# Three unread fp32 matmuls behind the modulation sums of the first two rows

## The chip, the cores and the metric

The kernel runs on one core of one Trainium2 chip. The time is device time in microseconds (us) of one launch. Of the kernel before there are three timed runs, and one more execution that was profiled; the rows below come from that one.

## The reference

One decoder layer over 512 positions of width 1024, in fp32. Its head, where the change sits, is this:

```python
mod = c @ w_ada[l] + b_ada[l]
sh1, sc1, gt1, sh2, sc2, gt2 = jnp.split(mod, 6, axis=-1)
h = rms_norm(x, g_pre_mix[l]) * (1.0 + sc1[:, None]) + sh1[:, None]
proj = h @ w_in[l]
```

Behind it come two groups of attention heads (one with compressed, selected and sliding-window branches, one with a top-k choice of keys), one output projection, a gated residual, a second modulated norm, and a squared-ReLU feed-forward of width 4096. Every value of the output depends on `proj`.

## The kernel before

The 1024 model columns are eight rows of 128, `k` = 0 to 7. For each row the head does the same things. The modulation weights of the row (`wm`, 1 MB) are loaded; PE multiplies them by the vector `c` (`mod_sums`, L286) into one PSUM bank, tile `mp`; ACT copies the partial sums to `macc` (L292); PE adds them up with two matmuls of one column each (`mod_mm`, L297), which write columns 256 and 257 of the same bank. DVE adds the bias (L301) and applies the norm's gain (L302): these are the row's scale and shift. With them ACT writes the high half of the modulated row, `hh` (L305); DVE computes the same row in full (L307) and subtracts `hh` from it, which gives the low half, `hl` (L308). The projection is done in three passes over high and low halves (`proj_pass`, L324): weights high (`uh`) with `hh`, weights low (`ul`) with `hh`, weights high with `hl`. The weights are halved by `split` (ACT at L123, DVE at L124). Two chunks of `w_in` columns run this way, A (452 columns, accumulators `pA`, four of them) and B (512 columns, `pB`, three of them, one row later). The first row's transposed input is `xT_0`; the others are made by PE transposes (`xTp`, L269) and copied by ACT or DVE (L270). Four of the transposes use the banks that `pA` takes over later.

The order on each engine is set by a scheduler that simulates the program with its own durations while the kernel is built. `tc.issue_after` holds an instruction behind another on its engine. Waits between engines are derived from the tiles; in the built program a reader of a PSUM bank waits for every matmul that the code writes into that bank ahead of it. The scheduler's order covers the whole program, so a change in the head can also move rows much later: the attention stage (about 100 to 390 us) mixes score matmuls (L886, L887), their row minima on DVE (L889, which free the four score banks), softmax scalings (L907), and the top-k search on DVE (MAX8 at L576, MATCH_REPLACE8 at L579, in rounds).

Of the kernel before, what the change touches and what calls it, by code (L numbers as in the profile page):

```python
# [69 lines left out]
def layer_kernel(  # L70
# [7 lines left out]
    V, A, G, PE, SY = nc.vector, nc.scalar, nc.gpsimd, nc.tensor, nc.sync  # L78
# [23 lines left out]
    def p2(name, dt=F32):  # L102
        return big.tile([P, 512], dt, tag="p2", name=name, bufs=N_P)
# [77 lines left out]
    ident = identr.bitcast(F32)  # L181
# [82 lines left out]
    xT = [p2(f"xT_{k}") for k in range(KT)]  # L264
# [29 lines left out]
    def mod_mm(k):  # L294
        ps, acc = macc[k]
        for v in range(2):
            mm = PE.matmul(ps[:, 256 + v:257 + v], acc[:, v, :], ones32, start=True, stop=True)  # L297
        return ps[:, 256:258], mm

    def mod_h(k, ps):  # L300
# [20 lines left out]
    def proj_pass(ps, t, k, w, n, i):  # L321
        hi, lo = w[k // 2]
        l, r = ((hh, hi), (hh, lo), (hl, hi))[i]
        return PE.matmul(ps[:, :n], l[:, t, k, :], r[:, k % 2, :n],  # L324
                         start=(k == 0 and i == 0), stop=(k == KT - 1 and i == 2))
# [8 lines left out]
    def behind(done, f, *args):  # L334

        with ExitStack() as es:
            for ins in done:
                es.enter_context(tc.issue_after(ins.ins))
            return f(*args)

    first = mod_sums(0)
    first_T = x_transpose(0, "S")
    mp, _ = mod_mm(0)
    behind((first, first_T), split_a, 0)
    rt_ops = rope_tables()
    psB = []
    for k in range(KT):
# [18 lines left out]
        for ps in (0, 1, 2):  # L366
            for t in range(NT):
                mm = proj_pass(psA[t], t, k, wA, 452, ps)
# [13 lines left out]
        if k + 1 < KT:  # L382
            mp, mm = behind((mm,), mod_mm, k + 1)
# [940 lines left out]
```

## Time and profile before

| what | value |
|---|---|
| median of three runs | 724.51 us (720.13 to 725.61) |
| profiled execution, its own time | 724.97 us |
| its span, first to last instruction | 723.2 us |
| mean granted TensorE clock | 0.967 |
| PE busy | 674.7 us (93%) |
| DVE busy | 510.3 us (71%) |
| ACT busy | 373.9 us (52%) |
| POOL busy | 191.9 us (27%) |

The span is 1.8 us shorter than the execution's own time, which also holds what lies around the first and last instruction. The granted clock is a share of full speed: 1.00 is 2.4 GHz and 0.50 is 1.2 GHz.

### The profile page before, as it was taken

To read this page: it belongs to the slowest core of one execution; us is meant where nothing else is said; L and a number is where in the kernel's file an instruction comes from. 1 tells how busy PE (TensorE), PEld (TensorE's weight loads), DVE (VectorE), ACT (ScalarE), POOL (GpSimd) and SP (SyncE) were. 2 spreads that over 40 slices of the span, in tenths; PEclk is the share of its full clock that TensorE was granted. 3 is DMA by queue.
4 is the path that set the end of the run, shared out by engine and by line. 5 is a ranking of instruction groups with operands and counts; after the bars stand their busy time and mean duration, and the time that the engine had idled before them with its cause. 6 is when DMAs were issued, how large, how long until landed. Compare 5 with 4: busy or idle time off the path is not lost.

```text
span 723.2 us, 10022 instructions
## 1 busy us (share of the span) xinstructions
PE 674.7 (93%) x3529; PEld 523.1 (72%) x3529; DVE 510.3 (71%) x1020; ACT 373.9 (52%) x755; POOL 191.9 (27%) x228
## 2 busy tenths in 40 slices
PE   3999989899998999799978999999999999999994
PEld 2678968777565676365668878888888888888883
DVE  5555458988997989775686539677597459695445
ACT  5343785435795669544464555433554355454221
POOL 3000285734523134222020022201140032231023
PEclk9899989999997999999999999999999999999998
DMA  9976630530316471462295212452144312322103
GB/s 293 311 232 188 199 88 1 117 116 30 118 30 191 133 171 30 117 233 87 65 339 156 90 54 85 145 178 57 29 146 146 116 30 58 88 88 93 53 1 116
DMA packets 91611, 87.15 MB, mean 121 GB/s; under 512 B 3909, under 2 KB 71593, under 8 KB 91562
## 3 DMA queue, kind: packets, MB, share of 16 engines
q1 hardware_dynamic: 91170, 86.46, 39.7%
q8 instruction: 28, 0.46, 0.3%
q14 instruction: 21, 0.17, 0.1%
q10 hardware_dynamic: 392, 0.06, 0.0%
HBM read 84.40 MB, written 2.10 MB: 120 GB/s over the span
## 4 chain that ended last, share of the span: by engine, by line
PE 74%; DVE 14%; DMA 4%; ACT 3%; POOL 2%; issue 2%; POOLq 0%; DVEq 0%; ACTq 0%; SPq 0%
PE up L1126 23%; PE dn L1254 15%; PE dn L1187 5%; PE op L1019 5%; PE pA L324 3%; PE O L918 3%; PE pB L324 2%; PE pj_E L324 2%; DVE wk L579 1%; PE pj_D L324 1%; DVE m L576 1%; DMA rwo_b<-in_w_out_dram 1%; DMA wg_g<-in_w_ada_dram 1%; PE tp_d L912 1%; PE pj_C L324 1%
## 5 line engine op out<-in xcount | busy, mean ns | idle before, releaser
L1126 PE MATMUL up<-hh,uh_U 128*128 128x512 f32 (+1 forms) x288 | 105.9, 369 | 3.2 <-ACT hh L123 2.7
L1126 PE MATMUL up<-hl,uh_U 128*128 128x512 f32 (+1 forms) x288 | 104.8, 369 | 1.0 <-DVE hl L124 1.0
L1126 PE MATMUL up<-hh,ul_U 128*128 128x512 f32 (+1 forms) x288 | 105.5, 368 | 0.0
L1216 POOL TENSOR_TENSOR r<-r,r 128x512 f32<-128x512 f32 x18 | 36.8, 2055 | 184.6 <-ACT r L1131 114.0
L123 ACT CAST th<-rd 128x1024 fp32r<-128x1024 f32 x42 | 44.2, 1053 | 75.1 <-PE dn L1254 40.6
L124 DVE TENSOR_TENSOR tl<-rd,th 128x1024 fp32r<-128x1024 f32 x42 | 53.9, 1288 | 39.4 <-ACT th L123 39.4
L124 DVE TENSOR_TENSOR ul_U<-rw_U,uh_U 128x1024 fp32r<-128x1024 f32 x32 | 43.1, 1346 | 32.8 <-ACT uh_U L123 32.6
L1126 PEld LDWEIGHTS up<-hh,uh_U 128*128 128x128 f32 x288 | 54.9, 191 | 12.7 <-ACT hh L123 3.2
L1126 PEld LDWEIGHTS up<-hl,uh_U 128*128 128x128 f32 x288 | 54.5, 191 | 10.0 <-DVE hl L124 1.2
L1126 PEld LDWEIGHTS up<-hh,ul_U 128*128 128x128 f32 x288 | 54.9, 191 | 8.7
L123 ACT CAST uh_U<-rw_U 128x1024 fp32r<-128x1024 f32 x32 | 33.6, 1049 | 50.9 <-PE up L1126 32.3
L1254 PE MATMUL dn<-th,sl 128*128 128x512 f32 x168 | 52.1, 391 | 0.3
L1254 PE MATMUL dn<-th,sh 128*128 128x512 f32 x168 | 51.9, 393 | 0.0
L1254 PE MATMUL dn<-tl,sh 128*128 128x512 f32 x168 | 51.7, 389 | 0.0
L1254 PEld LDWEIGHTS dn<-th,sh 128*128 128x128 f32 x168 | 31.5, 188 | 7.5 <-DVE usum L1241 0.6
L1254 PEld LDWEIGHTS dn<-th,sl 128*128 128x128 f32 x168 | 31.3, 188 | 7.6 <-DVE sl L124 1.2
L1254 PEld LDWEIGHTS dn<-tl,sh 128*128 128x128 f32 x168 | 31.5, 188 | 6.6
L1216 DVE TENSOR_TENSOR rd<-rd,rd 128x1024 f32<-128x1024 f32 x24 | 31.5, 1324 | 0.3
L123 ACT CAST sh<-r 128x512 fp32r<-128x512 f32 x42 | 25.2, 619 | 9.0 <-POOL r L1216 8.6
L124 DVE TENSOR_TENSOR sl<-r,sh 128x512 fp32r<-128x512 f32 x42 | 27.9, 710 | 0.0
L1241 DVE TENSOR_TENSOR y<-y,dn 128x512 f32<-128x512 f32 x40 | 25.5, 680 | 2.2 <-PE dn L1254 2.2
L576 DVE MAX8 m<-wk 128x8 f32<-128x256 f32 (+2 forms) x48 | 26.5, 552 | 0.7 <-POOL wk L571 0.4
(426 smaller groups left out, 1685.2 us busy)
## 6 DMA issues: line engine op xcount, KB each, us to landing
rw_U<-in_w_up_dram SPq DMA_DIRECT2D x32, 512.0 KB, 4.1
rd<-in_w_down_dram SPq DMA_DIRECT2D x24, 512.0 KB, 4.7
wm<-in_w_ada_dram SPq DMA_DIRECT2D x32, 256.0 KB, 6.1
x<-in_x_dram SPq DMA_DIRECT2D x8, 512.0 KB, 6.5
wv_g<-in_w_ada_dram SPq DMA_DIRECT2D x8, 512.0 KB, 6.9
rwo_a<-in_w_out_dram SPq DMA_DIRECT2D x16, 256.0 KB, 4.5
wv_a<-in_w_ada_dram SPq DMA_DIRECT2D x8, 512.0 KB, 4.0
rwo_b<-in_w_out_dram SPq DMA_DIRECT2D x16, 256.0 KB, 4.7
```

Source lines behind the costliest of these rows:

```text
L123: A.copy(hi, src)
L124: eng.tensor_tensor(lo, src, hi.bitcast(F32), op=OP.subtract)
L324: return PE.matmul(ps[:, :n], l[:, t, k, :], r[:, k % 2, :n], start=(k == 0 and i == 0), stop=(k == KT - 1 and i == 2))
L576: mx = V.max(m8, work[t])
L579: V.match_replace(work[t], m8, work[t], MARK)
L918: mm = [PE.matmul(O[j][g * 64:(g + 1) * 64, :], vn[kb][:, self.vsl[g]:self.vsl[g] + 64], pts[kb, g][0], start=(first and kb == 0), stop=(l ...
L1019: PE.matmul(stt["ps"], l[:, kk, :], r[:, kk % 2, :], start=(kk == 0 and i == 0), stop=(kk == 7 and i == 2))
L1126: PE.matmul(pv[:, t0:t1, :], l[:, k, :], r[:, t0:t1, k, :], start=(n == 0), stop=(n == 23))
L1187: PE.matmul(ps, l[:, t * P:(t + 1) * P], r[:, f % 2, :], start=(n == 0), stop=(n == 11))
L1216: eng.tensor_tensor(dst, x, y, op=op)
L1241: V.tensor_tensor(ya, ya, ps, op=op)
L1254: PE.matmul(ps[t], l[:, f, t * P:(t + 1) * P], r[:, f, :], start=(n == 0), stop=(n == 11))
```

## The change

After the two sums of rows 0 and 1, PE multiplies 252 columns of `xT_0` by the identity three times, in fp32, into columns 258 to 509 of the same bank. Nothing reads the result. `mod_mm` now returns the last of the three as its instruction, so what was issued behind the sum is issued behind that.

```diff
@@ -295,6 +295,10 @@
         ps, acc = macc[k]
         for v in range(2):
             mm = PE.matmul(ps[:, 256 + v:257 + v], acc[:, v, :], ones32, start=True, stop=True)
+        if k < 2:
+            with tc.issue_after(mm.ins):
+                for _ in range(3):
+                    mm = PE.matmul(ps[:, 258:510], ident, xT[0][:, 0:252], start=True, stop=True)
         return ps[:, 256:258], mm
```

From here on lines have numbers that are 4 higher in the changed kernel (L301 becomes L305).

The engines' orders move with it. First place: DVE in the head, from the first row's scale and shift to the second row's. Before:

```order
L301 TENSOR_TENSOR as_174<-mp_187,colb 128x2
L302 TENSOR_TENSOR as_174<-as_174,colT 128x1
L307 TENSOR_SCALAR h_0_213<-xT_164,as_174 128x512
L124 TENSOR_TENSOR ulA_207<-rwA_92,uhA_206 128x2x452
L308 TENSOR_TENSOR hl_173<-h_0_213,hh_172 128x4x128
L270 COPY xT_165<-xTp_217 128x512
L270 COPY xT_167<-xTp_229 128x512
L270 COPY xT_169<-xTp_280 128x512
L301 TENSOR_TENSOR as_174<-mp_255,colb 128x2
L302 TENSOR_TENSOR as_174<-as_174,colT 128x1
L124 TENSOR_TENSOR ulB_271<-rwB_175,uhB_270 128x1024
L307 TENSOR_SCALAR h_1_296<-xT_165,as_174 128x512
```

The same stretch of DVE after the change:

```order
L124 TENSOR_TENSOR ulA_210<-rwA_92,uhA_209 128x2x452
L305 TENSOR_TENSOR as_174<-mp_187,colb 128x2
L306 TENSOR_TENSOR as_174<-as_174,colT 128x1
L311 TENSOR_SCALAR h_0_216<-xT_164,as_174 128x512
L312 TENSOR_TENSOR hl_173<-h_0_216,hh_172 128x4x128
L270 COPY xT_165<-xTp_220 128x512
L270 COPY xT_167<-xTp_232 128x512
L270 COPY xT_169<-xTp_283 128x512
L124 TENSOR_TENSOR ulB_274<-rwB_175,uhB_273 128x1024
L305 TENSOR_TENSOR as_174<-mp_258,colb 128x2
L306 TENSOR_TENSOR as_174<-as_174,colT 128x1
L311 TENSOR_SCALAR h_1_302<-xT_165,as_174 128x512
```

In both rows the weights' low half (`ulA`, then `ulB`) now stands ahead of the add that makes the scale and shift; before it stood behind.

Second place: PE around the first row's sums. Before:

```order
L297 MATMUL mp_187<-ones_109,macc_196 128x1 x2
L324 MATMUL pA_235<-uhA_206,hh_172 128x452
L324 MATMUL pA_236<-uhA_206,hh_172 128x452
L324 MATMUL pA_235<-ulA_207,hh_172 128x452
L324 MATMUL pA_236<-ulA_207,hh_172 128x452
L324 MATMUL pA_235<-uhA_206,hl_173 128x452
```

PE there after the change:

```order
L297 MATMUL mp_187<-ones_109,macc_196 128x1 x2
L301 MATMUL mp_187<-xT_164,identr 128x252 x3
L328 MATMUL pA_238<-uhA_209,hh_172 128x452
L328 MATMUL pA_238<-ulA_210,hh_172 128x452
L328 MATMUL pA_239<-uhA_209,hh_172 128x452
L328 MATMUL pA_239<-ulA_210,hh_172 128x452
L328 MATMUL pA_238<-uhA_209,hl_173 128x452
```

The three unread matmuls stand between the sums and the first projection matmul, and two of the projection's matmuls change places; the second row gets the same three, with no other move on PE.

Third place: DVE at the start of the top-k search of the second query block (`wk` is the score table that is searched, `sk_kw` a split of window keys, `peT` a table that PE transposes for the compression). Before:

```order
L576 MAX m_1_1422<-wk_687 128x8
L579 MATCH_REPLACE wk_687<-m_1_1422,wk_687 128x256
L613 COPY peT<-pep_k 128x16
L576 MAX m_1_1449<-wk_687 128x8
L579 MATCH_REPLACE wk_687<-m_1_1449,wk_687 128x256
L576 MAX m_1_1476<-wk_687 128x8
L579 MATCH_REPLACE wk_687<-m_1_1476,wk_687 128x256
```

After:

```order
L580 MAX m_1_1428<-wk_693 128x8
L583 MATCH_REPLACE wk_693<-m_1_1428,wk_693 128x256
L580 MAX m_1_1455<-wk_693 128x8
L583 MATCH_REPLACE wk_693<-m_1_1455,wk_693 128x256
L580 MAX m_1_1482<-wk_693 128x8
L583 MATCH_REPLACE wk_693<-m_1_1482,wk_693 128x256
L617 COPY peT<-pep_k 128x16
```

Two rounds of the search have moved ahead of the copy of `peT`. Beyond these places the same instructions stand on every engine, with some dozens of rows in other places between about 100 and 390 us.

## Rows read from the trace of the kernel before

**Rows 1.** The page's part on the chain that ended last, by engine.

```profile
PE 74%; DVE 14%; DMA 4%; ACT 3%; POOL 2%; issue 2%; POOLq 0%; DVEq 0%; ACTq 0%; SPq 0%
```

**Rows 2.** The chain in the head: start us, us, what.

```profile
17.04 0.82 ACT hh L305
...
17.91 4.20 PE pA L324 x11
22.10 1.54 PE mp L286 x16
...
24.04 0.94 ACT uhB L123
...
26.24 3.19 PE pA L324 x8
...
30.67 0.59 PE xTp L269 x4
...
32.41 2.17 PE pB L324 x9
34.58 1.00 PE mp L286 x16
35.58 2.67 PE pA L324 x12
38.25 0.34 PE mp L297 x4
```

**Rows 3.** PE in order of time, head: start, us; idle before and its releaser.

```profile
17.91 0.94 PE L324 MATMUL pA<-uhA,hh 128*128 128x452 f32 x2 [2.22 <-ACT hh L305]
...
26.24 1.68 PE L324 MATMUL pA<-uhA,hh 128*128 128x452 f32 x4 [1.46 <-ACT hh L305]
```

**Rows 4.** Stretches of the head; the third column from the right is the granted clock.

```profile
19.60:19.70 0.10, 0.10 (x2) 0.00 (x0) 0.10 (x1) 0.00 (x0) 0.00 (x0) 0.82 1.09 277
23.00:23.10 0.10, 0.10 (x8) 0.08 (x4) 0.00 (x0) 0.00 (x0) 0.00 (x0) 0.61 1.17 349
26.40:26.50 0.10, 0.10 (x1) 0.10 (x2) 0.10 (x1) 0.00 (x0) 0.00 (x0) 0.95 1.11 348
29.80:30.00 0.20, 0.20 (x8) 0.17 (x4) 0.00 (x0) 0.00 (x0) 0.00 (x0) 0.74 1.15 289
```

**Rows 5.** DVE in order of time, head.

```profile
16.45 0.23 DVE L243 TENSOR_SCALAR rtab<-rtab 128x128 f32<-128x128 f32 x1
...
17.50 1.09 DVE L124 TENSOR_TENSOR ulA<-rwA,uhA 128x904 fp32r<-128x904 f32 x1
18.51 0.69 DVE L308 TENSOR_TENSOR hl<-h,hh 128x512 fp32r<-128x512 f32 x1
19.11 1.88 DVE L270 COPY xT<-xTp 128x512 f32<-128x512 f32 x3
...
25.16 1.23 DVE L124 TENSOR_TENSOR ulB<-rwB,uhB 128x1024 fp32r<-128x1024 f32 x1
```

**Rows 6.** PE at 179 us: two records of one full-width fp32 matmul.

```profile
179.49 1.02 PE L758 MATMUL gv_g<-bb,ones 128*128 128x512 f32 x2
```

**Rows 7.** A stretch with idle PE; columns as in rows 4, PE's busy time first.

```profile
369.90:385.00 15.10, 10.17 (x77) 9.04 (x76) 14.73 (x28) 7.68 (x18) 3.26 (x4) 1.00 0.81 255
```

**Rows 8.** DVE in the top-k search, in order of time.

```profile
107.76 0.43 DVE L576 MAX8 m<-wk 128x8 f32<-128x256 f32 x1 [0.40 <-POOL wk L571]
...
108.30 0.41 DVE L579 MATCH_REPLACE8 wk<-m,wk 128x256 f32<-128x256 f32 x1
...
111.75 0.17 DVE L613 COPY peT<-pep_k 128x16 f32<-128x16 f32 x1 [2.06 <-PE pep_k L611]
```

**Rows 9.** PE in the attention stage, behind two of its longer stalls.

```profile
144.58 0.50 PE L324 MATMUL pj_E<-uh_E,hh 128*128 128x512 f32 x1 [3.09 <-DVE mx L889]
...
221.36 0.44 PE L886 MATMUL s_s<-k1s,qC 128*128 128x384 f32 x1 [2.06 <-DVE mx L889]
```

**Rows 10.** Two stretches behind those stalls; columns as in rows 4.

```profile
146.00:149.30 3.30, 3.30 (x9) 2.52 (x9) 3.30 (x12) 0.86 (x4) 1.75 (x3) 0.50 0.01 2
...
224.50:234.70 10.20, 10.20 (x43) 6.20 (x40) 6.40 (x19) 4.22 (x10) 3.29 (x2) 0.50 0.70 228
```

## Prediction

> **What bounds the kernel.** I read the page's chain first: 74% of the span is PE [rows 1], so a shift of PE's work in the head goes on to the end unless a later stall swallows it. Then I followed the chain through the head. It runs PE, then the modulation chain, then PE, twice: hh of row 0 on ACT at 17.04, eleven projection matmuls from 17.91, the sums of row 1 from 22.10 to 23.64, the weights' cast on ACT to 24.98, and PE again at 26.24. From there it stays on PE [rows 2]. So there are just two gaps, of 2.22 and 1.46 us, and both end with hh [rows 3]. Last I looked at the granted clock: it falls from 1.00 to 0.50 (2.4 to 1.2 GHz) near 19.67, comes back near 23.06, falls again at 26.49 and is back by 29.9 [rows 4]. Each fall comes after one of the gaps, when PE is already at work again. The reader should see the price of the low clock: eight projection matmuls take 3.19 from 26.24, 0.40 each, twelve take 2.67 from 35.58, 0.22 each; the sums take 1.54 at 22.10 and 1.00 at 34.58 [rows 2].
>
> **The change, part by part.**
>
> *The unread matmuls themselves.* The nearest row is a full-width fp32 matmul of 512 columns: two records in 1.02, the second starting about 0.43 after the first, so 0.86 a matmul [rows 6]. 252 columns are 0.42, three are 1.27. The bounds are half of that, if the weights' second half cost nothing, and 2.5 at the low clock. I take 1.27, since the clock stands at 1.00 when both gaps begin. Row 0's three then run from about 15.6 to 16.9 and row 1's from 24.7 to 26.0, within PE's idle time [rows 3]. xT_0 is copied before the sums need their operand, so they add no new wait of PE's own, and no DMA moves in the head.
>
> *What they keep waiting.* They write the bank that DVE's add (L301) reads. In the built program the counter of PE that the add waits for is stepped by the third of them; before, the second sum stepped it. So the scale and shift of the row come behind all three. The Trainium skill has the rule behind this, in "PSUM — Partial Sum Buffer", section "PSUM bank collisions raise a hardware error": "Semaphore-guard PSUM by bank × quadrant (by bank is the simple version), not by address." By address the add would wait for the sums alone and the gaps would stay as they are; by the rule they grow. No run here shows the two side by side.
>
> *The first gap, +0.3.* The scheduler has put ulA ahead of the add (first place in the orders). DVE is busy with the angle tables until 16.68, and ulA takes 1.09 [rows 5]; it ends near 17.7, after the unread matmuls, and hides them. The add, hh and PE all come 1.09 later: hh at 18.13, PE at 19.0 in place of 17.91. If the unread matmuls ran at the low clock they would end near 18.2 and cost another 0.5. ulA no longer stands between hh and hl, so hl ends at 19.7 in place of 19.20 and the three xT copies, whose banks the third and fourth accumulators take, come 0.5 later, not 1.09 [rows 5]. What matters is that PE is idle from about 16.95 to 19.0: 2.05 us in place of 2.22. The idle time is moved, not removed. I therefore take the same fall of the clock at 19.67. Of the eleven matmuls three run before it, eight take 0.40 each, to 22.9; the sums begin at the low clock and end, with the clock back near 23.06, at 23.95. Before they ended at 23.64 [rows 2]. That is +0.3.
>
> *The second gap, +1.25.* ACT's cast of uhB ends at 24.98 [rows 2]; ulB (1.23, rows 5) now goes first, to 26.2, and then the add. From there to hh is about 0.4 (16.68 to 17.04 in row 0) and from hh to PE 0.87 (17.04 to 17.91) [rows 2, 5]: PE starts at 27.5 on the old axis in place of 26.24. The three unread matmuls end at 26.0 plus their drain, beside ulB. The idle time is 1.4, as before, but now a busy 1.27 stands ahead of it.
>
> *The clock behind the second gap, -1.57.* Before, row 1 took 6.17 from 26.24 to 32.41, most of it at the low clock. At the full one it is twelve matmuls 2.67, sums 1.00, transposes 0.59 and the small sums 0.34 [rows 2]: 4.60. Whether the clock stays up is the unknown; its price is 0 if it does not and -1.57 if it does. For it speaks a stretch of 15.10 us in which PE was busy for only 10.17 and the clock stayed at 1.00 [rows 7]; against it, that the same 1.46 brought a fall here [rows 3, 4]. I take the gain, for PE is now busy right before the gap.
>
> *The reordered attention stage, 0.* Two rounds of the search move ahead of the copy of peT, where DVE sat idle for 2.06 [rows 8]. A round is 0.43 and 0.41 with a load between, nearly 1 us, so two fill the idle time and nothing behind is later. Further on the moves go both ways. I take 0; the bounds are in the rivals. Few DMAs move there, and none that PE waits for in the rows read.
>
> The sum is +0.3 + 1.25 - 1.57 = -0.02 against the profiled execution's 724.97: **724.9 us**. The median of the three runs, 724.51, is 0.46 below that execution, well inside their spread of 5.5.
>
> **The rivals.**
>
> *The clock stays up through both gaps.* The Trainium skill ("TensorE: Matmul & The Clock Gate", section "Part 1: The HAM clock gate") says that "the default state is throttled, and activity releases the throttle"; by it the added work should keep the clock. As a mechanism of this kernel: the unread work until 16.9 and the early projection matmuls from 19.0 suffice, and 19.67 brings no fall. PE then waits for the first xT copy (20.2) and runs five matmuls at 0.22 to 21.3; the sums end at 22.3, 1.3 earlier than before. The sum is -1.3 + 1.25 - 1.57 = -1.6: **723.3**. Against it stands that the idle time is shortened by only 0.17.
>
> *The clock falls in both gaps.* Then only the later starts are left, +0.3 + 1.25: **726.5**. The mechanism is the filler plus ulB ahead of the add, and it decides if 1.4 us of idle still lowers the clock.
>
> *The order of the top-k search costs PE.* This is the other side. Ahead of the first row minimum (L889), which ends PE's stall of 3.09 [rows 9], DVE now has five more small search instructions at about 0.43 and one 0.28 fewer, some 2 us. They are paid by the idle 2.06 at 109.7 [rows 8]. If that idle time is gone, because the copy's operand comes sooner, PE's stall grows by up to 2.1, and another 3.4 us at the low clock, as after the stall before [rows 10], costs 1.7: **728.8**. It decides from the point where DVE no longer waits before the copy.
>
> *The order of the minima spares PE a stall.* Near 221, PE waits 2.06 [rows 9], and 10.20 us at the low clock follow [rows 10]. In the new order two of the minima that free banks there stand ahead of a group of scalings. If the stall and a part of the low clock go, up to 2.06 + 5.1: between 718 and 723, say **721**.
>
> **How the numbers follow.** Forecast 0.40, clock up in both 0.25, clock down in both 0.10, search order 0.13, order of the minima 0.12. The head's cases span 723.3 to 726.5; with the runs' own spread of some 2 us to each side, and most of the two order rivals, the range is 719 to 730. About 1% (7.2 us) is what a measurement of this kernel can tell from no change. None of the head's cases reaches it; only the ends of the order rivals do: faster by over 1% 0.05, slower 0.06, within 1% 0.89.
>
> **What would show it.** The add of row 0 near 17.7, ulA right before it, PE restarting at 19.0 with about 2 us of idle before; in row 1 ulB right before the add and some 1.4 idle; the clock at 0.50 near 20 to 23 but 1.00 from there past 30; the first row of pB near 32.4. The forecast is wrong if the unread matmuls take over 2 us, if the add runs beside them, if the clock falls behind the second gap, or if PE's stalls between 100 and 390 us add up to some 3 us more or less than before.

## The result, and the profile after

The changed kernel takes 726.98 us (median of 13 runs, 723.65 to 729.23). The kernel before, timed beside it, takes 721.66 (13 runs, 719.15 to 725.61). The ratio is 1.0072, with an interval of 1.0050 to 1.0094: 5.3 us slower by the medians, and still within 1%. The profiled execution of after has a span of 726.2 us at a mean granted clock of 0.972; before it was 723.2 at 0.967.

The chain that ended last, by engine, after. In this trace it can be followed back only to 107.69 us, so the shares add up to 85% (99% before, [rows 1]). PE's lower share is due to the missing start, and nothing is read from it.

```profile
PE 64%; DVE 14%; DMA 3%; issue 2%; POOL 1%; ACT 1%; DVEq 0%; POOLq 0%; ACTq 0%; SPq 0%
```

The head after, PE in order of time (start, length, engine, line, tiles, idle before and releaser). It answers to [rows 3].

```profile
16.69 0.50 PE L297 MATMUL mp<-ones,macc 128*128 128x1 f32 x4
17.06 1.52 PE L301 MATMUL mp<-xT,identr 128*128 128x252 f32 x6
20.14 0.47 PE L328 MATMUL pA<-uhA,hh 128*128 128x452 f32 x1 [1.56 <-ACT hh L309]
...
24.49 0.50 PE L297 MATMUL mp<-ones,macc 128*128 128x1 f32 x4
24.86 1.52 PE L301 MATMUL mp<-xT,identr 128*128 128x252 f32 x6
27.67 1.09 PE L328 MATMUL pA<-uhA,hh 128*128 128x452 f32 x4 [1.30 <-ACT hh L309]
```

DVE there, answering to [rows 5]: ulA and ulB now stand ahead of the add (L305), and both wait for ACT's cast.

```profile
17.81 1.10 DVE L124 TENSOR_TENSOR ulA<-rwA,uhA 128x904 fp32r<-128x904 f32 x1 [0.86 <-ACT uhA L123]
18.83 0.15 DVE L305 TENSOR_TENSOR as<-mp,colb 128x2 f32<-128x2 f32 x1
...
25.23 1.23 DVE L124 TENSOR_TENSOR ulB<-rwB,uhB 128x1024 fp32r<-128x1024 f32 x1 [2.62 <-ACT uhB L123]
26.41 0.16 DVE L305 TENSOR_TENSOR as<-mp,colb 128x2 f32<-128x2 f32 x1
```

The three stretches that can differ, after: from row 0's first small sum to the first pB matmul, from the first pj_C matmul to the first up matmul, and from there to the end. Behind the range stand its length, the busy time of PE, PEld, DVE, ACT and POOL, then the granted clock, the DMA share and GB/s.

```profile
16.69:32.19 15.50, 12.64 (x90) 9.14 (x89) 8.32 (x16) 6.69 (x11) 0.00 (x0) 1.00 1.13 317
92.30:364.47 272.17, 253.48 (x1439) 173.86 (x1437) 221.56 (x620) 167.45 (x425) 104.02 (x136) 0.95 0.39 106
364.47:726.24 361.77, 342.48 (x1585) 284.81 (x1583) 240.84 (x285) 160.05 (x233) 68.90 (x46) 0.98 0.32 100
```

The same three before:

```profile
15.18:32.27 17.09, 13.41 (x78) 9.00 (x77) 9.13 (x20) 6.59 (x11) 0.00 (x0) 0.80 1.13 316
92.39:365.04 272.65, 254.10 (x1438) 175.18 (x1437) 220.43 (x620) 167.46 (x425) 106.31 (x136) 0.94 0.37 106
365.04:723.17 358.13, 341.28 (x1585) 284.01 (x1583) 240.92 (x285) 160.40 (x233) 69.94 (x46) 0.99 0.32 101
```

The head got 1.59 shorter, with the clock at 1.00 all through it (0.80 before). The middle is 0.48 shorter. The last stretch is 3.64 longer. With 1.51 more ahead of row 0's small sums, where the two programs do the same, this is the whole difference of 3.07 between the spans. The loss between these two traces thus lies where nobody touched the kernel, behind 364 us. (It is 3.07 and not 5.3 because the profiled execution of before, 724.97, was itself 3.3 above the median of its 13 runs, and that of after, 728.09, only 1.1.) By the rows above, 2.44 of the 3.64 are idle time of PE and 1.20 busy time. DVE and PE at the place, before:

```profile
382.99 0.41 DVE L1067 TENSOR_SCALAR hq<-hp,col_a,col_sh 128x128 f32<-128x128 f32 x1
383.31 0.48 DVE L1058 TENSOR_SCALAR xn<-x,rs 128x512 f32<-128x512 f32 x1
383.70 0.68 DVE L124 TENSOR_TENSOR hl<-hq,hh 128x512 fp32r<-128x512 f32 x1
384.31 1.41 DVE L691 SCALAR_TENSOR_TENSOR acc_g<-wg_g,c_sb,acc_g 128x512 f32<-128x512 f32 x2
385.63 0.72 DVE L1067 TENSOR_SCALAR hq<-hp,col_a,col_sh 128x128 f32<-128x128 f32 x2
386.27 0.74 DVE L691 SCALAR_TENSOR_TENSOR acc_g<-wg_g,c_sb,acc_g 128x512 f32<-128x512 f32 x1
386.93 0.41 DVE L1067 TENSOR_SCALAR hq<-hp,col_a,col_sh 128x128 f32<-128x128 f32 x1
387.42 0.69 DVE L124 TENSOR_TENSOR hl<-hq,hh 128x512 fp32r<-128x512 f32 x1
389.40 0.75 DVE L691 SCALAR_TENSOR_TENSOR acc_g<-wg_g,c_sb,acc_g 128x512 f32<-128x512 f32 x1 [1.29 <-DMA wg_g<-in_w_ada_dram]
...
387.44 0.39 PE L1126 MATMUL up<-hh,uh_U 128*128 128x256 f32 x1 [2.50 <-ACT hh L123]
```

And after:

```profile
382.88 0.69 DVE L124 TENSOR_TENSOR hl<-hq,hh 128x512 fp32r<-128x512 f32 x1
383.48 1.57 DVE L695 SCALAR_TENSOR_TENSOR acc_g<-wg_g,c_sb,acc_g 128x512 f32<-128x512 f32 x2
384.96 0.41 DVE L1071 TENSOR_SCALAR hq<-hp,col_a,col_sh 128x128 f32<-128x128 f32 x1
385.28 0.48 DVE L1062 TENSOR_SCALAR xn<-x,rs 128x512 f32<-128x512 f32 x1
385.68 0.75 DVE L695 SCALAR_TENSOR_TENSOR acc_g<-wg_g,c_sb,acc_g 128x512 f32<-128x512 f32 x1
386.34 0.73 DVE L1071 TENSOR_SCALAR hq<-hp,col_a,col_sh 128x128 f32<-128x128 f32 x2
389.15 0.75 DVE L695 SCALAR_TENSOR_TENSOR acc_g<-wg_g,c_sb,acc_g 128x512 f32<-128x512 f32 x1 [2.08 <-DMA wg_g<-in_w_ada_dram]
389.81 0.41 DVE L1071 TENSOR_SCALAR hq<-hp,col_a,col_sh 128x128 f32<-128x128 f32 x1
390.13 0.74 DVE L695 SCALAR_TENSOR_TENSOR acc_g<-wg_g,c_sb,acc_g 128x512 f32<-128x512 f32 x1
390.79 1.29 DVE L124 TENSOR_TENSOR hl<-hq,hh 128x512 fp32r<-128x512 f32 x2
...
385.91 0.63 PE L1065 MATMUL hp<-identr,xn 128*128 128x128 f32 x4 [1.37 <-ACT hq L1073]
388.14 0.58 PE L1130 MATMUL up<-hh,uh_U 128*128 128x256 f32 x1 [1.61 <-ACT hh L123]
391.54 0.58 PE L1130 MATMUL up<-hl,uh_U 128*128 128x256 f32 x1 [1.31 <-DVE hl L124]
```

The last of the four row tiles of h2 is made in two halves, 30 and 31 (xn, hq, hl; `h2_steps(3)`). It shares DVE with the additions that build acc_g2 (`acc_steps`). Their sum is first read by PE at 422.3 us (L713, before), more than 30 us later. After, two of them stand ahead of the last part of hq_30 and of xn_31, and one that waits 2.08 us for its wg_g transfer stands ahead of the last part of hq_31. Before, that waiting addition stood behind it, ahead of one hl only. So PE stops three times (1.37, 1.61, 1.31) in place of once (2.50). The stretch at half the clock, which begins near the end of the second stop, is twice as long: 6.4 us in place of 3.2 in the rows below (after, then before; columns as above):

```profile
388.10:394.50 6.40, 5.04 (x22) 4.75 (x23) 2.94 (x5) 1.07 (x2) 0.00 (x0) 0.50 0.55 167
```

```profile
388.40:391.60 3.20, 3.20 (x17) 3.20 (x16) 2.02 (x3) 0.08 (x1) 0.00 (x0) 0.50 0.57 164
```

### The profile page after: what moved, and what is told of

It reads as the page before. It is cut to its first block, busy times and chain, and to the rows that moved or that the text cites. A ratio compares the mean times of both kernels' runs of the same rounds, so it can differ in the third digit from the quotient of the medians.

```text
span 726.2 us, 10047 instructions
## 1 busy us (share of the span) xinstructions
PE 675.9 (93%) x3541; PEld 523.4 (72%) x3541; DVE 512.0 (71%) x1020; ACT 373.9 (51%) x755; POOL 188.5 (26%) x228
## 4 chain that ended last, share of the span: by engine, by line
PE 64%; DVE 14%; DMA 3%; issue 2%; POOL 1%; ACT 1%; DVEq 0%; POOLq 0%; ACTq 0%; SPq 0%
PE up L1130 22%; PE dn L1258 15%; PE op L1023 6%; PE dn L1191 5%; PE O L922 3%; PE pj_E L328 3%; DMA wg_g<-in_w_ada_dram 2%; DVE wk L583 2%; DVE m L580 2%; PE tp_s L916 1%; PE tp_d L916 1%; DVE P_d L911 1%; DMA rwo_b<-in_w_out_dram 1%; PE tp_w L916 1%; DVE acc_g L695 1%
```

## The experiments

Theory A: this order on DVE near 385 us, called the late order below, costs 3 us or more. Rival B: the unread matmuls, and the waits that they make in the head, cost the 5.3. Rival C: the new order of the top-k searches and of the attention stages costs it. The three come apart because the scheduler, given another number of matmuls or one edge, writes other orders. Times are medians; ratios are to runs of the kernel before on the same chip, whose median was 721.55 to 722.83 beside the experiments. A ratio can differ by 0.2% from that of the two medians (e4: 1.0023 against 1.0046; e7: 1.0000 against 0.9982), so a difference of less than 2 us between single kernels decides little. Head and last are the first and third stretch above, from each kernel's own profile.

| kernel | matmuls per row | searches, attention | late order | head us, clock | last us | us | ratio, interval |
|---|---|---|---|---|---|---|---|
| before | 0 | before | before | 17.09, 0.80 | 358.13 | 721.66 | 1 |
| after | 3 | after | after | 15.50, 1.00 | 361.77 | 726.98 | 1.0072, 1.0050 to 1.0094 |
| e1_six | 6 | before | before | 17.83, 1.00 | 358.40 | 725.59 | 1.0039, 1.0017 to 1.0061 |
| e2_none_new_order | 0 | after | after | 18.40, 0.72 | 361.36 | 727.58 | 1.0075, 1.0047 to 1.0103 |
| e3_four | 4 | nearly after | before | 16.14, 1.00 | 358.87 | 724.83 | 1.0040, 1.0015 to 1.0065 |
| e4_five | 5 | a third | after | 17.01, 1.00 | 361.24 | 725.49 | 1.0023, 0.9999 to 1.0047 |
| e5_late_pinned | 3 | after | before | 15.49, 1.00 | 357.97 | 724.33 | 1.0047, 1.0024 to 1.0070 |
| e6_narrow | 3 of 8 columns | the third | before | 16.99, 0.90 | 357.75 | 722.58 | 1.0029, 1.0002 to 1.0057 |
| e7_none_row1 | 0 | the third | before | 19.51, 0.83 | 358.18 | 720.28 | 1.0000, 0.9973 to 1.0028 |
| e8_before_again | 0 | before | before | 13.68, 1.00 | 357.69 | 721.49 | 1.0004, 0.9976 to 1.0032 |
| e9_additions_last | 0 | before | additions last | 14.88, 0.89 | 354.56 | 718.15 | 0.9947, 0.9925 to 0.9969 |
| e10_row1_additions_last | 0 | the third | additions last | 15.60, 0.89 | 354.70 | 716.34 | 0.9936, 0.9913 to 0.9959 |
| e11_change_additions_last | 3 | after | additions last | 15.49, 1.00 | 355.34 | 721.28 | 0.9992, 0.9973 to 1.0012 |
| e12_none_late_pinned | 0 | after | before | 14.26, 1.00 | 357.09 | 724.31 | 1.0011, 0.9983 to 1.0038 |

**e1_six.**

```diff
-                for _ in range(3):
+                for _ in range(6):
```

> Six unread matmuls in each of the two rows instead of three; behind the two rows every engine has the order of the kernel before again. Theory A (the cost lies at 383 to 392 us, where the new order puts additions of acc_g2 that wait for wg_g transfers ahead of hq_30, xn_31 and hq_31): the head takes some 3 us more than after's (2 rows x 3 x 0.51 us, which the add waits for), the clock stays up in the two gaps, the late cost is gone: 723 us (721 to 725). Theory B (the matmuls and the waits they make in the head cost the 5.3 us): twice the work, 730 to 733. Theory C (the new order of the top-k searches and of the attention stages costs it): as A, 723.

725.59, above A's range by 0.6 and far from B's 730 to 733: twice the matmuls cost less than three. The last stretch is back at 358.40. The head takes 2.33 more than after's, because here the add does wait for the matmuls. DVE in e1:

```profile
19.40 0.16 DVE L305 TENSOR_TENSOR as<-mp,colb 128x2 f32<-128x2 f32 x1 [0.98 <-PE mp L301]
...
28.26 0.16 DVE L305 TENSOR_TENSOR as<-mp,colb 128x2 f32<-128x2 f32 x1 [1.23 <-PE mp L301]
```

**e2_none_new_order.** The kernel before with one edge: row 0's add is held behind `lows[0]`, ulA's subtraction.

```diff
...
-        V.tensor_tensor(as1[:, :, k], ps, colb[:, :, k], op=OP.add)
+        with ExitStack() as es:
+            if k == 0:
+                es.enter_context(tc.issue_after(lows[k].ins))
+            V.tensor_tensor(as1[:, :, k], ps, colb[:, :, k], op=OP.add)
...
```

> No unread matmul at all: the kernel before with one edge that keeps row 0's addition behind ulA's subtraction; from the top-k searches on, DVE, ACT and POOL have the order of after. A: the late cost is there without any matmul, the clock falls in the gaps as before: 726 to 728. B: as before, 722 (721 to 723). C: 727, as A, but with the loss ahead of 369 us in the trace.

727.58, as slow as the changed kernel, without one unread matmul. B has fallen as far as it names the matmuls; the order is enough. One wait of the head, row 0's add behind ulA, is still in this kernel.

**e3_four** and **e4_five.** `range(4)` and `range(5)` in place of `range(3)`.

> Four unread matmuls in each row; the searches and the attention stages in after's order, hq_30, xn_31, hq_31 and the additions of acc_g2 in the order of before. A: 721.5 us (720 to 723.5). B: 728 to 730. C: 727 to 728.

> Five unread matmuls in each row; the order ahead of the pj_E stall as in before, a third order in the attention stages, and hq_30, xn_31, hq_31 and the additions of acc_g2 as in after. A: the late cost is back: 726 us (724.5 to 728). B: 730. C: 722 to 723, the stall ahead of pj_E at 3.1 us.

The last stretch follows the late order alone: 358.87 in e3, 361.24 in e4. The times don't follow A as well: e3 came out 1.3 over A's upper end, and e4, with the costly late order, at 725.49, within A's range but hardly above e3. Its middle is short, from the first pj_C to the first up matmul (e4):

```profile
93.17:359.68 266.51, 250.21 (x1439) 173.15 (x1437) 223.32 (x620) 167.56 (x425) 106.71 (x136) 0.97 0.40 108
```

That is 6.1 less than before, with PE busy for 3.9 less and a clock of 0.97 in place of 0.94. So a part of C is true in a form that I had not written down: the order of the attention stages does move the time, and this third one makes it shorter. The middle takes 266.51 to 269.71 in the four traces of the third order (e4, e6, e7, e10) and 270.14 to 273.29 in the four of before's (before, e1, e8, e9). After's order is not the longer one: 271.11 to 272.42 in four traces (after, e2, e5, e11), with e12 apart at 276.67.

**e5_late_pinned.** The change, with DVE's late order of before (one hl stands earlier). `h2[3, 1]` is the instruction that makes xn_31, `h2[3, 0, "l"]` the one that makes hl_30.

```diff
-                        eng.scalar_tensor_tensor(av, ...)
+                        es = ExitStack()
+                        late = None if nm != "g2" else h2[3, 0, "l"] if (half, i) == (1, 3) else h2[3, 1] if (half, i) == (0, 3) or (half, i, a) == (1, 2, 1) else None
+                        if late is not None:
+                            es.enter_context(tc.issue_after(late.ins))
+                        with es:
+                          eng.scalar_tensor_tensor(av, ...)
...
```

> The changed kernel with its three unread matmuls; edges keep the last five additions of acc_g2 behind xn_31, hq_31 and hl_30, which gives DVE there the order of the kernel before; all else as in after. A (the late order costs 3.0 to 3.6 us, by the stretch from the first up matmul to the end: 361.2 to 361.8 us in three kernels that have it, 358.1 to 358.9 in three that have not): that stretch back at 358 to 359, the time 723 to 724 us, 3.3 under after's. B (matmuls and their waits in the head): 727, unchanged. C (order of searches and attention stages): 727.

The last stretch is 357.97, 3.80 under after's, and the time 724.33: 2.65 of the 5.3 us are gone. PE stops once there, as before (e5):

```profile
385.43 0.39 PE L1135 MATMUL up<-hh,uh_U 128*128 128x256 f32 x1 [2.27 <-ACT hh L123]
```

The trace shows A for this half. The times alone would not, as the two intervals overlap (1.0050 to 1.0094 and 1.0024 to 1.0070); e12 against e2 and e11 against after, below, say the same with intervals that do not. The other half, a ratio of 1.0047, is not the late order's.

**e6_narrow.** `ps[:, 258:266]` and `xT[0][:, 0:8]` in place of the 252 columns.

> The three unread matmuls in each of the two rows with 8 columns instead of 252, so that they take next to no time; the late order is that of before, the order of the attention stages is the one of e4_five. A, with the attention order of e4_five taken as 2 us better: 720 us (718 to 722). B: as before, 722. C: 722 if that order costs nothing, 724 to 726 if any new order costs.

722.58, half a us over A's range. The head tells more: PE goes on 3.45 us behind row 0's first small sum and 3.13 behind row 1's, as with 252 columns (3.45 and 3.18). In the changed kernel the matmuls hide beside ulA and ulB; what PE pays for is that ulA and ulB stand ahead of the add. PE in e6:

```profile
16.07 0.50 PE L297 MATMUL mp<-ones,macc 128*128 128x1 f32 x4
16.44 0.81 PE L301 MATMUL mp<-xT,identr 128*128 128x8 f32 x6
19.52 0.48 PE L328 MATMUL pA<-uhA,hh 128*128 128x452 f32 x1 [2.26 <-ACT hh L309]
```

**e7_none_row1.** e2's edge with `if k == 1`, that is behind ulB.

> No unread matmul; the kernel before with one edge that keeps row 1's addition behind ulB's subtraction. Late order of before, attention order of e4_five. A: the edge costs up to 1.2 us in the head, the attention order gives 2: 721 us (719 to 723). B: the wait that the edge makes in row 1 is one of the changed kernel's, half of 5.3: 724 to 725. C: 722, or 724 to 726 if any new order costs.

720.28 with a ratio of 1.0000: the edge lengthens row 1's gap to 2.64 us and the head to 19.51, and the middle, 267.50 in the third order of the attention stages against 272.65, makes up for it.

**e8_before_again.**

> The kernel before, unedited, for a second profile of it. If the clock's falls in the two gaps of the head are a matter of the execution, one or both are missing here, and the stretch from the first row's sums to the first pB matmul takes 13.7 to 15.4 us instead of 17.09; if the gaps always bring them, it takes 17.1 again. The last stretch 358 to 359 us.

The first gap is 0.47 us shorter than in [rows 3], at 1.75; the second is the same, at 1.45. The clock stays up behind both, and the head takes 13.68 in place of 17.09 (e8):

```profile
15.79:29.47 13.68, 10.48 (x79) 7.16 (x77) 8.70 (x19) 6.58 (x11) 0.00 (x0) 1.00 1.13 318
```

e2 and e12 make the case stricter. Their heads are the same, with the same two gaps, 2.94 and 1.46 us; the clock was 0.72 in one execution and 1.00 in the other, and the head took 18.40 and 14.26. Whether a gap of this length lowers the clock is a matter of the execution. The first gaps, e2, then e12:

```profile
20.45 0.75 PE L327 MATMUL pA<-uhA,hh 128*128 128x452 f32 x1 [2.94 <-ACT hh L308]
...
19.22 0.47 PE L327 MATMUL pA<-uhA,hh 128*128 128x452 f32 x1 [2.94 <-ACT hh L308]
```

**e9_additions_last**, **e10_row1_additions_last**, **e11_change_additions_last.** The last six additions of acc_g2 behind hl_31 (`h2[3, 1, "l"]`), in before, in e7 and in the changed kernel.

```diff
...
+                        late = None if nm != "g2" or (half, i) not in ((1, 2), (0, 3), (1, 3)) else h2[3, 1, "l"]
...
```

> The kernel before (no unread matmul) with edges that put the last six additions of acc_g2 behind hl_31. A (additions ahead of hq_30, xn_31, hq_31 and hl_31 are what PE waits for there): four additions of 0.66 us and the wait of 1.3 to 1.5 us for a wg_g transfer leave the chain; PE's stop of 2.5 us ahead of the up matmuls shrinks to 1 to 2 us, the stretch from the first up matmul to the end goes from 357.7 or 358.1 to 356.5 to 357.3, the time 721 us. Rival D: the additions free the buffers later that the rw_U loads behind them in SP's queue need, and PE waits for ul_U instead: that stretch 359 to 361, the time 723 to 725.

> e7_none_row1 with the same edges: no unread matmul, row 1's addition behind ulB's subtraction, the last six additions of acc_g2 behind hl_31. A: 1 us under e7_none_row1, 719 to 720, which would be the fastest of all. D: 722 to 724.

> The changed kernel, three unread matmuls in two rows, with the same edges. A: 1 us under e5_late_pinned, 723; still over the kernel before, by the 1.2 us that each of the first two rows takes longer with the addition behind ulA or ulB. D: 725 to 727.

All three beat what A expected. Rival D, that PE would wait for buffers that come free later, has fallen: the last stretch is 354.56 to 355.34, where D had 359 to 361. e9 is the kernel before without its own share of the same fault: 0.53% faster. e10 is the fastest version of all, 0.64% under before. e11 brings the changed kernel back to before's time. In e9 PE's stop is down to 0.97, and behind it the clock no longer falls (PE, DVE; then the stretch that follows):

```profile
384.36 0.39 PE L1131 MATMUL up<-hh,uh_U 128*128 128x256 f32 x1 [0.97 <-ACT hh L123]
...
387.14 2.73 DVE L696 SCALAR_TENSOR_TENSOR acc_g<-wg_g,c_sb,acc_g 128x512 f32<-128x512 f32 x4
...
388.00:395.00 7.00, 7.00 (x60) 7.00 (x60) 4.65 (x6) 3.86 (x6) 0.00 (x0) 1.00 0.58 163
```

The last stretch of 354.56 is 3.6 under the 358.13 of before: 2.05 less idle time of PE in it, 1.5 of it at this stop, and 1.5 less busy time, about half of the 3.2 us that ran at half the clock before.

**e12_none_late_pinned.** e2 with e5's edges.

> e2_none_new_order with the edges of e5_late_pinned: no unread matmul, row 0's addition behind ulA's subtraction, the searches and the attention stages in after's order, the last five additions of acc_g2 as in before. If the order of the searches and the attention stages costs the 2 to 2.8 us by which e5_late_pinned is over before: row 0's edge 0.7 to 1.2 and that, 724.5 to 725.5. If it costs nothing, and e5's rest is the head's: 722.3 to 723. Either way the stretch from the first up matmul to the end at 357.7 to 358.9, some 3 us under e2's 361.4.

The last stretch is 357.09 against e2's 361.36, and the time 724.31 against 727.58: A a second time, without the matmuls, and with intervals that do not overlap. Over all fourteen traces the last stretch goes by the late order alone: 361.24 to 361.77 with after's, 357.09 to 358.87 with before's, 354.56 to 355.34 with the additions last. On the rest of e5 e12 decides little. Its median lies just under the range for a cost of the searches' order, its ratio of 1.0011 (up to 1.0038) is nearer to none, and its own trace has a middle 4.3 us longer than e2's, which has the same order of the searches there.

## Why the prediction was right and where it was wrong

The time, 726.98, lies in the range of 719 to 730, and within 1% of before, as forecast. The number of the forecast, 724.9, was near by luck: it stands on the profiled execution's 724.97, which lay 3.3 above the median of 13 runs. The change itself was forecast as -0.02 and measured as 5.3.

*The step that failed* is "The reordered attention stage, 0". The argument "further on the moves go both ways" was never taken past 235 us. Behind 364 us the same kind of move put additions that nobody needs yet, one of them waiting for a transfer, ahead of a chain that PE waits for. Its size is 3.6 us between the first two traces (4.08 against e8), and 3.8 and 4.3 where it was taken out (after to e5, e2 to e12); in the medians 2.65 and 3.3. No rival held it.

*The unread matmuls and what waits for them.* Right in mechanism. Three were priced at 1.27 and took 1.52, the second half of it beside ulA. That the add waits for the last of them, and not for the sums that it reads, e1 shows with 0.98 and 1.23. The rule of the Trainium skill ("PSUM — Partial Sum Buffer", section "PSUM bank collisions raise a hardware error"), to guard by bank and not by address, agrees with this.

*The two gaps.* PE goes on 3.45 us behind row 0's first small sum; it was 2.73 before, 2.25 in e8 and 1.93 in e9. For row 1 it is 3.18 against 1.97. That is 0.7 to 1.5 and 1.21, where I had 1.09 for the start and 1.25. In row 0 the reason was only half seen: I let the angle tables decide when ulA begins, but DVE then waits another 0.86 for ACT's cast (0.36 in e5). The two first small sums before:

```profile
15.18 0.50 PE L297 MATMUL mp<-ones,macc 128*128 128x1 f32 x4
...
24.27 0.50 PE L297 MATMUL mp<-ones,macc 128*128 128x1 f32 x4
```

*The clock in the head.* The first gap was forecast to bring the fall again. It did not; the clock was at 1.00 in the whole head, as its row above shows, and so at all four places of [rows 4].

So the rival with the clock up in both gaps was right in mechanism, and its -1.6 is what the two first traces show for the head (-1.59), part by part: -1.29 from row 0's small sums to row 1's, where it had -1.3, and -0.30 from there to pB, where it had +1.25 - 1.57. The full clock holds beyond the one pair: all six profiles with three or more full-length matmuls have the head at 1.00; of the eight without, six have it at 0.72 to 0.90, among them e6, which has three short ones and in which PE goes on as late as in after. The Trainium skill's "activity releases the throttle" ("TensorE: Matmul & The Clock Gate", Part 1) agrees. But the gain was priced against an execution that had both falls. Against e8, which had none, the same head is 1.82 slower. The three traces with before's head (before, e8, e9) have 17.09, 13.68 and 14.88, 15.2 on average; after, e5 and e11 have 15.5. Over these the matmuls keep the clock up, and the later starts eat what that gives.

*The rivals of order.* Both of their stalls moved as described, and at once. The stall ahead of pj_E [rows 9] grew from 3.09 to 4.71:

```profile
145.27 0.55 PE L328 MATMUL pj_E<-uh_E,hh 128*128 128x512 f32 x1 [4.71 <-DVE mx L893]
...
219.34 0.44 PE L890 MATMUL s_s<-k1s,qC 128*128 128x384 f32 x1 [0.77 <-DVE mx L893]
```

The one near 219 went from 2.06 to 0.77. Over the middle the two traces differ by 0.48 us, so neither won. The sign that I had named, some 3 us more or less of PE's stalls between 100 and 390, did not show either: PE's idle time in the middle is 18.69 against 18.55, and the three stops behind 385 add 1.79, the last of them behind 390.

*What stays open.* With the late order taken out, the change is still 2.8 us slower than the runs of before beside it (e5, 724.33 against 721.55), and 3.1 slower with the additions last (e11 against e9). The two later starts in the head account for up to 1.8 of it, less what the clock gives back, which differs by execution. The traces do not show this rest: the spans of e11 and e9 are 718.14 and 718.60, those of e5 and e8 721.15 and 720.56, so each pair is within 0.6. Whether it belongs to the order of the searches, e12 could not settle. A kernel with the matmuls in which the add stays ahead of ulA and ulB was not tried.

## What to carry to other kernels

When a scheduler writes the order, compare the whole order, and at each place where it changed ask which engine's wait ends there, above all where work that nobody needs yet, or that waits for a transfer, moves ahead of a short chain that feeds TensorE. Such work is best tied behind the chain by an edge: it was worth 0.5% to the kernel before, and had no part in the forecast. And take a second profile of the kernel before, before pricing a gain of the clock: of its two, one had stretches of the head at half speed and the other had none.

## What was not expected of the hardware

- The same head with the same two gaps (2.94 and 1.46 us) had a granted clock of 0.72 in one execution (e2) and 1.00 in another (e12), and took 18.40 and 14.26 us.
- In e9, a stop of 0.97 us in place of 2.50 was followed by a clock of 1.00 where before 0.50 had followed, so that an edge that takes 1.5 us out of one stop shortened the last stretch by 3.6.
- Three fp32 matmuls (six records) with 8 columns took 0.81 us, with 252 columns 1.52: 31 times the columns take less than twice the time. By a straight line through the two, an estimate, 0.79 of the 0.81 does not go with the columns.
